# A kernel whose gate tiles get their Silu from the hyperbolic tangent, and whose Fourier row buffers share three rooms

## The chip, the cores and the metric

The kernel runs on one core of a Trainium2 chip. A core has a matrix engine (TensorE, PE in the profile, with its weight loads shown apart as PEld), a vector engine (VectorE, DVE), an engine for functions of single elements (ScalarE, ACT), a general one (GpSimd, POOL) and one that mostly issues transfers (SyncE, SP). Each runs its own instructions in order; semaphores join them. On-chip memory has 128 partitions (SBUF), and products are summed in PSUM banks. The metric is device time in microseconds of one execution; lower is better.

## The reference

Two sequences (prompt and sample) of 1024 rows and 1024 columns, fp32, go through one encoder layer. What matters here, for each sequence:

```python
xn = rmsnorm(x, g_pre)
p = xn @ w_in
fv, fg, hv, hg, mg = jnp.split(p, ...)
fz = jnp.fft.fftn(fz, axes=(1, 3), norm="ortho").real   # fz: fv in 4 groups of 256
y_f = (fz * jax.nn.silu(fg)) @ w_fourier_out
...                                                     # z: two gated long convolutions of hv
y_h = (z.astype(dt) * jax.nn.silu(hg)) @ w_hyena_out
g_f, g_h = jnp.split(jax.nn.sigmoid(mg + b_merge), 2, axis=-1)
out = (g_f * y_f + g_h * y_h) @ w_out
return x + rmsnorm(out, g_post)
```

`silu(x)` is x / (1 + exp(-x)), which is also x * (tanh(x/2) + 1) / 2. The long convolutions use filters of two orders that a small network makes: a product with sines, times an exponential decay, normed by the sum of absolute values, then taken to the frequency domain.

## The kernel before

Every fp32 matrix product is made of pairs: a number is split into a high part `h` and a rest `l`, both in the type float32r, and three products (h by h, l by h, h by l) are summed in PSUM (`mm3`; all products show up as L194). Weights that are split on the fly come in halves of 128 x 512: `wr` is read, ACT writes `h` (L761) and minus `h` (L762), and a transfer that adds, issued on POOL's queue, brings the weight again to make `l` (L763). `rooms` (L724) gives the halves of four tiles in turn a place: two pairs of rooms `wh`/`wl`, the room `draw`, and the room `draw2` of the pool `stage2`; in the last two a half is called `whl`.

The program has four stages. In the **Fourier stage** (0 to about 270 us) the sequences are normed, projected and transformed, one after the other. For each sequence four times a pair of row buffers, A and B (L458 and L459), is filled by DVE in four pieces each (L480 to L485) from the PSUM tile pQ and from Ps and Pm, copies of pP that ACT makes (L475, L476). POOL's queue then writes A and B to memory as `d_fz` (L486, L487). A and B have one buffer each, so the next pair waits for this transfer to end. In the first sequence the same places hold the first two input rows (L317). Ps, Pm and another small tile, `sev`, lie last in this stage's pool `ff`.

In the **filter stage** (about 225 to 720 us, begun while the Fourier stage ends) the filters' taps are made (L619 on: pft and the norm pn on PE, `ex` with Exp and Abs on ACT, T on DVE) and taken to the frequency domain (pXf). In between, `spill_gate` (L792) projects the gates: pairs of PSUM tiles pin0 and pin1 of 48 products of 512 columns in all. Section 0, the Fourier gate, is multiplied at once by `fz`, read back from `d_fz`; other sections are copied. The result goes to memory (`d_g`).

In the **convolution stage** (to about 1740 us) each channel block is projected, transformed, multiplied and transformed back; for some blocks the second gate is read back from `d_g` into `sg` and put through Silu (L1008). The table `cinv` of the inverse transform is read (L940) on POOL's queue when the Fourier stage's rooms are free. In the **block stage** (to the end) the output projections are made; its order is written by hand.

The order in the other stages is set by the program's scheduler: it simulates all instructions with a table of costs and puts each where the simulated engines are free. So an edit in one place can move work far away. The rooms of a pool follow one another in memory, and a pool that is closed gives its memory to the next ones, which wait for its last use.

Of the kernel before, what the change touches and what calls it, by code (L numbers as in the profile page):

```python
# [9 lines left out]
F32 = mybir.dt.float32  # L10
F32R = mybir.dt.float32r
I32 = mybir.dt.int32
AF = mybir.ActivationFunctionType
# [3 lines left out]
P = 128  # L17
D = 1024
# [143 lines left out]
class K:  # L162
# [143 lines left out]
    def norm(self, b, px, pf):  # L306

        nc, a = self.nc, self.a  # L310
        ss = px.tile([P, 8], F32, tag="ss", name=f"ss{b}")
        self.rs = rs = px.tile([P, 8], F32, tag="rs", name=f"rs{b}")
        self.diag = dg = px.tile([P, 8, P], F32, tag="dg", name=f"dg{b}", bufs=1)
        self.xs = []
        for m in range(8):
            if b == 0 and m < 6:
                x = pf.tile([P, D], F32, tag=("fA", "fB", "ee0", "ee1", "oo0", "oo1")[m], name=f"x0_{m}", bufs=1)  # L317
            else:
                x = px.tile([P, D], F32, tag="x", name=f"x{b}_{m}", bufs=3)
            nc.sync.dma_start(x, a[f"x{b}"][m * P:(m + 1) * P, :])  # L320
            self.xs.append(x)
            sq = px.tile([P, D], F32, tag="xg", name="sq", bufs=2)
            self.squared = nc.scalar.activation(sq, x, AF.Square, accum_out=ss[:, m:m + 1])
            if m % 4 == 3:
                q = slice(m - 3, m + 1)
                self.rstd(px, rs[:, q], ss[:, q], 4)
                for j in range(m - 3, m + 1):
                    self.scaled = nc.vector.tensor_scalar(dg[:, j], self.ident, rs[:, j:j + 1], None, op0=MUL)
# [57 lines left out]
    def fourier_half(self, b, half, W, fo, px, pf, begun={}):  # L386

        nc = self.nc
        WE, WO = W

        def pair(shape, tag, bufs=1):
            return [pf.tile(shape, F32R, tag=f"{tag}{i}", name=f"{tag}{i}", bufs=bufs) for i in range(2)]
        EE, OO = pair([P, 4, 260], "ee"), pair([P, 4, 256], "oo")
        for e, (W_, n, X_) in enumerate(((WE, 260, EE), (WO, 256, OO))):
            for m in range(4):
                p = begun.get((e, m))
                if p is None:
                    p = self.psum("mm", 4, f"pfv{e}")
                    for k in range(8):
                        self.pfv(p, e, m, k, W, fo)  # L400
                self.split(X_[0][:, m], X_[1][:, m], p[:, :n], "dve", "act")
                if e == (b + half == 0):

                    if m == 0:
                        p5 = self.psum("X", 2, "pfx")[0:36, :260]
                    for k in (2 * m, 2 * m + 1):
                        for i in range(2):
                            self.mm(p5, fo["x5"][:, k], WE[i][:, k], k + i == 0, k + i == 8)

        X5, XX, PX = fo["x5t"], fo["xx"], fo["px"]  # L410
        nc.scalar.copy(X5[0:36], p5)
        self.sub("dve", X5[32:36], p5[32:36], X5[32:36])

        EX = fo["ex"]
        for i in range(2):
            for g in range(2):
                nc.vector.tensor_copy(EX[i][:, :, g:g + 33:32], EE[i][:, :, 130 * g + P:130 * g + P + 2])
        for g in range(2):
            nc.vector.tensor_copy(XX[0:36, g:g + 33:32], X5[0:36, 130 * g + P:130 * g + P + 2])
        seq = fo["seq"].rearrange("p h (e m c) -> p h e m c", e=2, m=4)  # L420
        al = fo["alt"][:, b * 86:b * 86 + 86].unsqueeze(1).to_broadcast([P, 3, 86])

        def stage(np_, data, e, edge, out, tag):

            pe = self.psum(tag, 2, "pse")[0:np_, :258]
            po = self.psum(tag, 2, "pso")[0:np_, :258]
            for m in range(4):
                last = (edge is None and m == 1) or m == 3
                self.mm3(pe if m < 2 else po, data(m), (seq[:, 0, e, m], seq[:, 1, e, m]), m % 2 == 0, last)
                if m == 1 and edge is not None:  # L430
                    self.mm(pe.rearrange("p (a b) -> p a b", a=3), edge, al, False, True)
            ev = pf.tile([P, 258], F32, tag="sev", name="sev", bufs=1)[0:np_]
            st = pf.tile([P, 514], F32, tag="sst", name="sst", bufs=1)[0:np_]
            nc.scalar.copy(ev, pe)
            self.add("dve", st[:, 0:258], ev, po)
            if e == 0:
                self.sub("dve", st[:, 512:257:-1], ev[:, 0:255], po[:, 0:255])
            else:
                self.stt("dve", st[:, 512:257:-1], ev[:, 0:255], -1.0, po[:, 0:255])
            nc.vector.tensor_copy(st[:, 513:514], st[:, 0:1])  # L440
            if len(out) == 2:
                self.split(out[0], out[1], st, "dve", "act")
            else:
                nc.scalar.copy(out[0][0:34], st)
                self.sub("dve", out[0][32:34], st[32:34], out[0][32:34])
        ch, cx = fo["chan"], fo["chx"]
        vec = self.vec
        PP = []
        for g in range(2):
            cs = slice(130 * g, 130 * g + P)  # L450
            PP.append(pair([P, 514], "pp", 2))
            stage(P, lambda m: (EE[0][:, m, cs], EE[1][:, m, cs]), 0, X5[:, cs], PP[g], "TX"[g])
        stage(34, lambda m: (EX[0][:, m], EX[1][:, m]), 0, XX, [PX], "T")
        for g in range(2):
            Pp, Qp = PP[g], pair([P, 514], "qp")
            co = slice(P * g, P * g + P)
            stage(P, lambda m: (OO[0][:, m, co], OO[1][:, m, co]), 1, None, Qp, "XT"[g])
            A = pf.tile([P, 1026], F32, tag="fA", name="fA", bufs=1)  # L458
            B = pf.tile([P, 1026], F32, tag="fB", name="fB", bufs=1)  # L459
            gg = 2 * half + g  # L460
            for n in range(2):
                w = (258, 256)[n]
                ns = slice(258 * n, 258 * n + w)
                pr, qr = (Pp[0][:, ns], Pp[1][:, ns]), (Qp[0][:, ns], Qp[1][:, ns])
                pP = self.psum("X", 2, "pP")[:, :w]
                self.mm3(pP, (ch[:, 0, 0:P], ch[:, 1, 0:P]), pr, True, False)
                self.mm(pP, cx[:, 0, g, :], PX[:, ns], False, True)
                pQ = self.psum("X", 2, "pQ")[:, :w]
                self.mm3(pQ, (ch[:, 0, P:2 * P], ch[:, 1, P:2 * P]), qr, True, False)
                self.mm(pQ, ch[:, 0, 2 * P:3 * P], pr[0], False, False)  # L470
                self.mm(pQ, ch[:, 0, 2 * P:3 * P], pr[1], False, False)
                self.mm(pQ, cx[:, 1, g, :], PX[:, ns], False, True)
                Ps = pf.tile([P, 258], F32, tag="fPs", name="fPs", bufs=2)
                Pm = pf.tile([P, 258], F32, tag="fPm", name="fPm", bufs=1)
                nc.scalar.copy(Ps[:, :w], pP)  # L475
                nc.scalar.activation(Pm[:, :w], pP, AF.Copy, scale=vec[:, 11:12])  # L476
                t0 = 258 * n
                w = (258, 255)[n]
                r = slice(0, w)
                self.stt("dve", A[:, t0:t0 + w], pQ[:, r], vec[:, 10:11], Ps[:, r])  # L480
                self.add("dve", B[:, t0:t0 + w], pQ[:, r], Pm[:, r])
                w = (258, 254)[n]
                r = slice(0, w)
                self.stt("dve", A[:, 1024 - t0:1024 - t0 - w:-1], pQ[:, r], vec[:, 11:12], Ps[:, r])
                self.stt("dve", B[:, 1024 - t0:1024 - t0 - w:-1], pQ[:, r], vec[:, 12:13], Pm[:, r])  # L485
            nc.gpsimd.dma_start(self.d_fz[b][2 * gg], A[:, 0:1024])  # L486
            nc.gpsimd.dma_start(self.d_fz[b][2 * gg + 1], B[:, 0:1024])  # L487

# [303 lines left out]
    def spill_gate(self, b, sec, ct, ws):  # L792
# [4 lines left out]
        for n in range(2):  # L797
            s = slice(512 * n, 512 * n + 512)
            t = self.wp.tile([P, 512], F32, tag="gt", name="gt", bufs=3)
            if sec:  # L800
                nc.scalar.copy(t, ps[n])
            else:
                f = self.wp.tile([P, 512], F32, tag="gt", name="fz", bufs=3)
                nc.sync.dma_start(f, self.d_fz[b][ct][:, s])
                nc.scalar.activation(t, ps[n], AF.Silu)
                self.mul("dve", t, t, f)
            nc.sync.dma_start(self.d_g[b][sec][ct][:, s], t)


# [707 lines left out]
```

## Time and profile before

| | us |
|---|---|
| three executions | 2432.15, 2436.44 (median), 2437.8 |
| the profiled execution | 2433.46 |
| its span in the trace | 2431.7 |
| busy: PE | 2365.3 (97%) |
| busy: DVE | 1984.6 (82%) |
| busy: ACT | 1182.4 (49%) |
| busy: POOL | 452.5 (19%) |

The spans and windows below are in microseconds from the span's start. A row of the timeline gives the start, the duration, the engine, the line, the operation with output and inputs, and in brackets how long the engine was idle before it and what ended that. "Granted clock" is the share of TensorE's full clock that the chip allowed in a window. A busy PE is not always a PE at its peak, so the distance from one product to the next is looked at as well.

### The profile page before, as it was taken

What the parts mean: (1) busy time and instruction counts of PE and PEld (TensorE: products, weight loads), DVE (VectorE), ACT (ScalarE), POOL (GpSimd) and SP (SyncE); (2) the same over time, 40 slices, a digit from 0 to 9 for tenths busy, and PEclk for the clock granted to TensorE, in tenths of its full rate; (3) what the DMA queues carried; (4) which work ended last, traced back from release to release, by engine and by line L of the source; (5) the groups of instructions that cost most, each with busy time, mean ns of one, the idle gap of its engine ahead of it and who ended that gap; (6) DMA issues with size and microseconds to landing.
All of it is one profiled execution on the core that took longest, in us unless ns stands there. A gap on an engine that the chain in (4) does not pass through costs nothing. (4 is left out here: it accounts for less than half of the span.)

```text
span 2431.7 us, 37263 instructions
## 1 busy us (share of the span) xinstructions
PE 2365.3 (97%) x13006; PEld 2052.9 (84%) x13006; DVE 1984.6 (82%) x3840; ACT 1182.4 (49%) x2224; POOL 452.5 (19%) x568
## 2 busy tenths in 40 slices
PE   5998999999989999999999999999999999999998
PEld 5988888888878888888888888888878888888786
DVE  7687577777768999999899999997666687777777
ACT  5545677766765444434232332333344475656543
POOL 1331111111122222221025544410000000101000
PEclk9999999999989999999999999999999999999999
DMA  8546877777768667766455666554546687888744
GB/s 320 166 165 209 244 199 207 200 201 196 217 186 239 194 199 202 205 177 186 146 181 193 211 218 215 192 170 135 207 150 228 211 301 253 268 269 231 219 156 156
DMA packets 262981, 499.65 MB, mean 205 GB/s; under 512 B 26551, under 2 KB 90264, under 8 KB 262409
## 3 DMA queue, kind: packets, MB, share of 16 engines
q1 hardware_dynamic: 220076, 380.53, 47.6%
q0 software_dynamic: 42528, 116.72, 18.6%
q8 instruction: 102, 1.67, 0.3%
q14 instruction: 87, 0.70, 0.1%
q10 hardware_dynamic: 188, 0.02, 0.0%
HBM read 333.59 MB, written 167.77 MB: 206 GB/s over the span
## 5 line engine op out<-in xcount | busy, mean ns | idle before, releaser
L194 PE MATMUL pin<-xh,wh 128*128 128x512 f32 x1024 | 402.6, 394 | 1.7 <-DVE v L177 1.1
L194 PE MATMUL pin<-xl,wh 128*128 128x512 f32 x1024 | 402.5, 393 | 0.0
L194 PE MATMUL pin<-xh,wl 128*128 128x512 f32 x1024 | 401.8, 394 | 0.0
L194 PE MATMUL pin<-xh,whl 128*128 128x512 f32 x896 | 289.8, 393 | 0.0
L194 PEld LDWEIGHTS pin<-xh,wh 128*128 128x128 f32 x1024 | 193.7, 189 | 37.6 <-DVE v L177 1.4
L194 PEld LDWEIGHTS pin<-xh,wl 128*128 128x128 f32 x1024 | 193.6, 189 | 35.5
L194 PEld LDWEIGHTS pin<-xl,wh 128*128 128x128 f32 x1024 | 193.8, 189 | 34.9
L194 PE MATMUL pT<-cinv,yh 128*128 128x256 f32 x1024 | 192.6, 282 | 1.9 <-ACT xt L821 1.9
L194 PEld LDWEIGHTS pin<-xh,whl 128*128 128x128 f32 x896 | 166.5, 188 | 32.8
L194 PE MATMUL pin<-xl,whl 128*128 128x512 f32 x448 | 176.4, 394 | 0.0
L194 PEld LDWEIGHTS pT<-cinv,yh 128*128 128x128 f32 x1024 | 163.9, 190 | 11.0 <-ACT xt L821 2.3
L194 PE MATMUL pX<-bh,cfwd 128*128 128x256 f32 x768 | 160.5, 286 | 1.1 <-DVE t L181 1.0
L181 DVE TENSOR_TENSOR t<-pX,k 128x1024 f32<-128x1024 f32 x128 | 155.9, 1218 | 5.1 <-PE pX L194 2.6
L171 ACT CAST yh<-y 128x512 fp32r<-128x512 f32 x128 | 79.4, 620 | 149.5 <-DVE y L181 132.0
L194 PE MATMUL pT<-cinv,yl 128*128 128x256 f32 x512 | 145.2, 284 | 0.2 <-DVE yl L181 0.2
L171 ACT CAST bh<-b 128x512 fp32r<-128x512 f32 x144 | 88.8, 618 | 106.8 <-DVE b L181 76.6
L181 POOL TENSOR_TENSOR draw<-draw 128x256 f32<-128x256 f32 x96 | 112.1, 1168 | 108.9 <-DMA draw<-d_sh 38.3
L194 PEld LDWEIGHTS pX<-bh,cfwd 128*128 128x128 f32 x768 | 125.9, 190 | 4.7 <-DVE t L181 1.2
L181 DVE TENSOR_TENSOR bl<-b,bh 128x512 fp32r<-128x512 f32 x144 | 101.6, 707 | 22.3 <-ACT bh L171 22.1
L194 PE MATMUL pX<-bl,cfwd 128*128 128x256 f32 x384 | 109.7, 286 | 0.0
L177 DVE SCALAR_TENSOR_TENSOR x<-pin,wsh,x 128x512 f32<-128x512 f32 (+1 forms) x128 | 90.6, 743 | 11.4 <-ACT x L783 11.2
L194 PEld LDWEIGHTS pT<-cinv,yl 128*128 128x128 f32 x512 | 97.6, 191 | 2.5 <-DVE yl L181 0.4
(367 smaller groups left out, 6070.3 us busy)
## 6 DMA issues: line engine op xcount, KB each, us to landing
k<-d_k SPq DMA_DIRECT2D x128, 512.0 KB, 4.5
wr<-in_w_in SPq DMA_DIRECT2D x136, 256.0 KB, 3.6
d_g<-gt SPq DMA_DIRECT2D x92, 256.0 KB, 3.7
d_k<-kt SPq DMA_DIRECT2D x128, 128.0 KB, 3.0
d_k<-kt SPq DMA_DIRECT2D x64, 256.0 KB, 3.1
fz<-d_g SPq DMA_DIRECT2D x64, 256.0 KB, 5.4
wl<-in_w_in POOLq DMA_DIRECT2D x56, 256.0 KB, 5.3
whl<-in_w_in POOLq DMA_DIRECT2D x56, 256.0 KB, 5.1
```

Source lines behind the costliest of these rows:

```text
L171: self.rounded = nc.scalar.copy(h, src)
L177: self.nc.vector.scalar_tensor_tensor(out, a, s, b, op0=op0, op1=op1)
L181: return e.tensor_tensor(out, a, b, op=op)
L194: return self.nc.tensor.matmul(out, lhsT, rhs, start=start, stop=stop, skip_group_check=shared)
```

## The change

```diff
--- before.py
+++ after.py
@@ -314,7 +314,7 @@
         self.xs = []
         for m in range(8):
             if b == 0 and m < 6:
-                x = pf.tile([P, D], F32, tag=("fA", "fB", "ee0", "ee1", "oo0", "oo1")[m], name=f"x0_{m}", bufs=1)
+                x = pf.tile([P, D], F32, tag=("fAB", "fAB", "ee0", "ee1", "oo0", "oo1")[m], name=f"x0_{m}", bufs=3 if m < 2 else 1)
             else:
                 x = px.tile([P, D], F32, tag="x", name=f"x{b}_{m}", bufs=3)
             nc.sync.dma_start(x, a[f"x{b}"][m * P:(m + 1) * P, :])
@@ -455,8 +455,8 @@
             Pp, Qp = PP[g], pair([P, 514], "qp")
             co = slice(P * g, P * g + P)
             stage(P, lambda m: (OO[0][:, m, co], OO[1][:, m, co]), 1, None, Qp, "XT"[g])
-            A = pf.tile([P, 1026], F32, tag="fA", name="fA", bufs=1)
-            B = pf.tile([P, 1026], F32, tag="fB", name="fB", bufs=1)
+            A = pf.tile([P, 1026], F32, tag="fAB", name="fA", bufs=3)
+            B = pf.tile([P, 1026], F32, tag="fAB", name="fB", bufs=3)
             gg = 2 * half + g
             for n in range(2):
                 w = (258, 256)[n]
@@ -802,8 +802,9 @@
             else:
                 f = self.wp.tile([P, 512], F32, tag="gt", name="fz", bufs=3)
                 nc.sync.dma_start(f, self.d_fz[b][ct][:, s])
-                nc.scalar.activation(t, ps[n], AF.Silu)
-                self.mul("dve", t, t, f)
+                nc.scalar.activation(t, ps[n], AF.Tanh, scale=0.5)
+                self.stt("dve", t, t, 1.0, ps[n], ADD, MUL)
+                self.stt("dve", t, t, 0.5, f, MUL, MUL)
             nc.sync.dma_start(self.d_g[b][sec][ct][:, s], t)
```

The row buffers and the first two input rows have one tag, `fAB`, with three buffers instead of two tags with one each. The tiles of the pool behind them lie 4128 bytes per partition higher. In the gate tiles of section 0, ACT computes tanh(p/2) instead of silu(p); DVE then makes (t + 1) * p, with p from PSUM, and t * 0.5 * fz, where it made one product before. The Silu of the convolution stage stays.

The matrix products are the same in number and kind, and the program has 7 instructions ACT_TABLE_LOAD, where it had 25. The scheduler puts many instructions elsewhere. Three places follow.

POOL at the end of the Fourier stage, before, the numbers being those of the program's tiles (`whl_3612` is the second half of the second gate tile; `d_fz1` the rows of the second sequence):

```order
L763 DMA whl_3582<-in_w_in 128x512
L763 DMA whl_3612<-in_w_in 128x512
...
L486 DMA d_fz1_0_101<-fA_2827 128x1024
L487 DMA d_fz1_1_102<-fB_2828 128x1024
L763 DMA whl_3965<-in_w_in 128x512
L763 DMA wl_4004<-in_w_in 128x512
L486 DMA d_fz1_2_103<-fA_2895 128x1024
L487 DMA d_fz1_3_104<-fB_2896 128x1024
L763 DMA wl_4035<-in_w_in 128x512
L940 DMA cinv_4071<-in_c_inv 128x6144
L763 DMA whl_4284<-in_w_in 128x512
```

And in the changed program:

```order
L763 DMA whl_3582<-in_w_in 128x512
...
L763 DMA wl_3659<-in_w_in 128x512
L763 DMA wl_3690<-in_w_in 128x512
L763 DMA whl_3937<-in_w_in 128x512
L486 DMA d_fz1_0_101<-fA_2827 128x1024
L487 DMA d_fz1_1_102<-fB_2828 128x1024
L486 DMA d_fz1_2_103<-fA_2895 128x1024
L487 DMA d_fz1_3_104<-fB_2896 128x1024
L941 DMA cinv_4073<-in_c_inv 128x6144
L763 DMA whl_3612<-in_w_in 128x512
```

The transfer for `whl_3612` stood ahead of the second sequence's row buffers, and stands behind the last of them and behind `cinv`. The places of the tiles in memory show why: `sev`, Ps and Pm lay below the room `draw2`, and now overlap it.

PE behind the last pQ of the Fourier stage (`pQ_2922`), before: 40 projection products of other tiles stand between the first pft and pn (the first and the last two are shown):

```order
L194 MATMUL pQ_2922<-px_281,chx_287 128x256
L194 MATMUL pft_3040<-w3s_2993,hid_2985 128x256 x2
L194 MATMUL pin1_3655<-xh0_5_3069,wl_3688 128x512
L194 MATMUL pin1_3655<-xh0_6_3074,wh_3687 128x512
...
L194 MATMUL pin0_3933<-xl0_6_3075,whl_3965 128x512
L194 MATMUL pin0_3933<-xh0_6_3074,whl_3965 128x512
L652 MATMUL pn_3057<-acc_3001,ones_73 128x128
L653 MATMUL pn_3057<-ones_73,acc_3001 128x2
```

And in the changed program:

```order
L194 MATMUL pQ_2922<-px_281,chx_287 128x256
L194 MATMUL pft_3040<-w3s_2993,hid_2985 128x256 x2
L652 MATMUL pn_3057<-acc_3001,ones_73 128x128
L653 MATMUL pn_3057<-ones_73,acc_3001 128x2
L194 MATMUL pft_3104<-w3s_3095,hid_2985 128x256 x2
L194 MATMUL pft_3116<-w3s_3095,hid_2985 128x256 x2
L194 MATMUL pft_3104<-w3s_3095,hid_2985 128x256 x2
L194 MATMUL pft_3116<-w3s_3095,hid_2985 128x256 x2
L194 MATMUL pin0_3580<-xh0_4_3064,whl_3612 128x512
L194 MATMUL pin0_3580<-xl0_4_3065,whl_3612 128x512
L194 MATMUL pin1_3581<-xh0_4_3064,whl_3612 128x512
L194 MATMUL pin1_3581<-xl0_4_3065,whl_3612 128x512
```

Four products with the high part of `whl_3612` stand among the taps; behind them come four and one of pXf, the next filter's spectrum, and then the other twenty products with `whl_3612`, ten for each of pin0 and pin1, which need its low part too. Before, 90 projection products stood between `pQ_2922` and that spectrum.

ACT near the end of the filter stage, where the convolution stage's first gates come back from memory, before (`ex_7541` belongs to the last filter but one):

```order
L640 ACTIVATE ex_7541<-dec_7509,vec_68 128x256 x2
L1008 ACT_TABLE_LOAD
L1008 ACTIVATE sg_9154<-sg_9154 128x512
L171 CAST bh_7598<-b2_7589 128x512
L761 CAST wh_8677<-wr_8679 128x512
L171 CAST bh_7609<-b1_7590 128x512
L1008 ACTIVATE sg_9790<-sg_9790 128x512
```

And in the changed program (`ex_7908` and `ex_7921` belong to the last filter):

```order
L640 ACTIVATE ex_7908<-dec_7876,vec_68 128x256 x2
L801 COPY gt_8357<-pin0_8295 128x512
L171 CAST bh_7965<-b2_7956 128x512
L171 CAST bh_7976<-b1_7957 128x512
...
L1009 ACT_TABLE_LOAD
L1009 ACTIVATE sg_9166<-sg_9166 128x512
L640 ACT_TABLE_LOAD
L640 ACTIVATE ex_7921<-dec_7876,vec_68 128x256 x2
L1009 ACT_TABLE_LOAD
L1009 ACTIVATE sg_9170<-sg_9170 128x512
L695 ACTIVATE kt2_7999<-pXf_7988,th_69 128x128
```

The table loads and Silus of the first `sg` tiles stood ahead of the casts bh of the last filter but one; now they stand one filter later, behind two of the casts bh and between two Exp. On PE, between the pn that precedes the last filter's taps and its last pft, 49 projection products stood and 78 stand; the convolution stage starts its first product with 1632 of the projections' products done instead of 1702.

## The prediction

> **What bounds the kernel now.** I read the busy time by windows first, because the mean over the span mixes stages. Its columns are the stretch, then busy time (instructions) of PE, PEld, DVE, ACT and POOL, the granted clock, the DMA share and GB/s.
>
> ```profile
> 180.00:240.00 60.00, 52.28 (x381) 49.07 (x380) 43.86 (x94) 34.63 (x69) 13.14 (x18) 0.94 0.60 195
> 240.00:660.00 420.00, 420.00 (x2262) 362.47 (x2261) 308.62 (x789) 293.36 (x643) 55.03 (x66) 1.00 0.76 209
> 660.00:720.00 60.00, 51.55 (x242) 42.67 (x241) 45.07 (x113) 38.51 (x81) 12.66 (x19) 0.89 0.71 199
> 715.00:1740.00 1025.00, 1020.80 (x6034) 903.59 (x6033) 942.83 (x1698) 372.56 (x660) 281.22 (x332) 1.00 0.62 191
> 1380.00:1440.00 60.00, 60.00 (x364) 53.51 (x364) 59.67 (x108) 17.96 (x33) 33.61 (x37) 1.00 0.65 215
> ```
>
> The filter stage (240 to 660), where the gate tiles are made, is PE's: 420.00 of 420.00 us busy at full clock, with ACT at 293 and DVE at 309. Time is lost at its two ends: 7.7 us without PE work in 180 to 240 and 8.5 in 660 to 720, both with a clock below 1. The view of waits names what ended the idle time there (total, times, longest); first row from 200 to 240, the others from 672 to 722:
>
> ```profile
> PE pQ L194 <- DVE fB L177: 6.1, 1, 6.1
> PE pXf L194 <- ACT bh L171: 3.7, 1, 3.7
> PE pft L194 <- DVE T L181: 3.6, 3, 2.4
> PE pin L194 <- DVE v L177: 1.1, 1, 1.1
> ```
>
> So the change can move time only where PE idles now, or where it makes PE idle anew.
>
> **The gate's arithmetic: 0.** These are the groups by line:
>
> ```profile
> L640 ACT ACT_TABLE_LOAD x11 | 14.1, 1283 | 0.1
> L805 ACT ACT_TABLE_LOAD x8 | 10.3, 1283 | 0.1
> L805 ACT ACTIVATE gt<-pin 128x512 f32<-128x512 f32 x16 | 9.6, 597 | 0.1
> L177 DVE SCALAR_TENSOR_TENSOR x<-pin,wsh,x 128x512 f32<-128x512 f32 (+1 forms) x128 | 90.6, 743 | 11.4 <-ACT x L783 11.2
> L181 DVE TENSOR_TENSOR gt<-gt,fz 128x512 f32<-128x512 f32 x48 | 33.2, 692 | 17.8 <-ACT gt L805 13.1 <-DMA fz<-d_fz 3.5
> ```
>
> Now 25 loads of ACT's function table are made; the listing of the changed program has 7, since Tanh needs no load beside the filters' Exp. The 18 that go are 18 x 1283 ns = 23.1 us of ACT. DVE gets one scalar_tensor_tensor more for each of 16 halves; the nearest row with a PSUM operand of 128x512 is 743 ns, and the second one takes the place of the multiply of 692 ns: 16 x (743 + 743 - 692) = 12.7 us. Both lie below PE's 420 of 420: ACT's 293 falls, DVE's 309 grows to about 321. The PSUM bank is released by DVE instead of ACT, some 0.7 us later; four banks turn and half a tile of 24 products takes 5.5 us (0.23 us each, the pitch shown further down), so this hides as well. Without that cover the DVE work would cost 12.7 us. I take 0, between -2 and +3.
>
> [...]
>
> **The row buffers: -4.** The second pair of the second sequence, DVE and PE in order of time (start, duration, and in brackets the idle time before and its releaser), then two windows:
>
> ```profile
> 215.30 0.49 DVE L177 SCALAR_TENSOR_TENSOR fA<-pQ,vec,fPs 128x258 f32<-128x258 f32 x1 [4.23 <-DMA d_fz<-fA]
> 217.68 0.43 DVE L181 TENSOR_TENSOR fB<-pQ,fPm 128x258 f32<-128x258 f32 x1 [1.89 <-DMA d_fz<-fB]
> 218.96 1.01 PE L194 MATMUL pQ<-qp,chan 128*128 128x256 f32 x3 [6.09 <-DVE fB L177]
> 215.00:220.00 5.00, 1.04 (x5) 1.04 (x6) 1.70 (x4) 1.00 (x2) 0.00 (x0) 0.53 0.77 270
> 220.00:225.00 5.00, 4.17 (x26) 3.58 (x26) 3.88 (x9) 4.27 (x9) 1.05 (x2) 0.79 0.37 137
> ```
>
> PE waits 6.09 us for a PSUM bank that DVE cannot empty, because A and then B still wait for their old contents to be written out. With three rooms the second A has a free one. The second B takes the first A's room, so it still needs that transfer, which let A start at 215.30; B then starts behind it instead of at 217.68. That is 2.4 us for certain. If the room is free before PE gets there, all 6.09 goes, with the slow clock behind it (1.05 us by 5 x 0.21 in the second window): 7.1. Work queued on ACT behind the Pm copy (the hidden layer's and the taps' casts, then x5t) starts earlier too, but some of it waits for weights. I take -4 of (-2.4, -7.1).
>
> **The fourth weight room: +19.** The Fourier pool grows by 4128 bytes, and its last tiles (sev, Ps, Pm) now lie on the room `draw2`, which was free before. The second half of the second gate tile, whl_3612, cannot be filled until the stage's last read of Pm. In the changed order its accumulating transfer stands on POOL's queue behind the last two row buffers and behind `cinv`. That queue before, the last pQ on PE, and two answers on transfers from 270 to 300 and 240 to 330:
>
> ```profile
> 268.09 0.28 PE L194 MATMUL pQ<-px,chx 128*128 128x256 f32 x1
> 270.45 0.56 POOL L487 DMA_DIRECT2D d_fz<-fB  x1
> 277.45 0.55 POOL L940 DMA_DIRECT2D cinv<-in_c_inv  x1 [4.27 <-DMA d_fz<-fB]
> 277.99 0.92 POOL L763 DMA_DIRECT2D whl<-in_w_in  x1
> cinv<-in_c_inv POOLq DMA_DIRECT2D x1, 3072.0 KB, 12.9
> DMA to landing us min/median/max: 4.3/6.0/14.2
> ```
>
> Before, a weight half is issued at the same place, 277.99; nothing on PE needs it soon: 90 products of tiles whose weights are there stand between the last pQ and the next filter's spectrum. Now four stand there, and the twenty that follow need the late half's low part. From the end of the last pQ (268.4) to the issue is 9.6 us, and to its landing 23.8 us with the longest landing of 14.2 (the one behind cinv has that neighbour) or 15.6 with the median of 6.0. PE has in between, by the changed order, 18 products pft and two pn, four with the high half and five of pXf: about 4 us at 0.23 us for 512 columns and half of that for 256. Idle time is then 11.6 to 19.8 us. The restart is slow: thirteen products at 0.43 us instead of 0.23 (rows of the next part) add 2.6. Bounds +14 and +22; since the neighbour cinv is the same, I take +19. Whether DVE and ACT go on with the taps meanwhile does not pay PE back at once: it was already full from 240 to 660.
>
> [...]
>
> **The end of the filter stage: -12.** ACT and PE in order of time:
>
> ```profile
> 672.42 0.64 ACT L1008 ACTIVATE sg<-sg 128x512 f32<-128x512 f32 x1 [2.79 <-DMA sg<-d_g]
> 676.92 1.28 ACT L1008 ACT_TABLE_LOAD   x1 [1.05 <-DMA sg<-d_g]
> 678.75 0.60 ACT L171 CAST bh<-b 128x512 fp32r<-128x512 f32 x1
> 679.41 0.54 PE L194 MATMUL pXf<-bh,cfwd 128*128 128x256 f32 x1 [3.74 <-ACT bh L171]
> 681.03 0.63 PE L194 MATMUL pin<-xh,wl 128*128 128x512 f32 x1
> 681.45 0.63 PE L194 MATMUL pin<-xh,wh 128*128 128x512 f32 x1
> 706.09 0.51 PE L194 MATMUL pft<-w3s,hid 128*128 128x256 f32 x2 [2.42 <-DVE T L181]
> 711.37 0.80 PE L194 MATMUL pin<-xh,wh 128*128 128x512 f32 x1 [1.07 <-DVE v L177]
> 711.96 0.63 PE L194 MATMUL pin<-xl,wh 128*128 128x512 f32 x1
> 712.39 0.63 PE L194 MATMUL pin<-xh,wl 128*128 128x512 f32 x1
> 717.29 0.39 PE L194 MATMUL pin<-xh,wl 128*128 128x512 f32 x1
> 717.53 0.39 PE L194 MATMUL pin<-xh,wh 128*128 128x512 f32 x1
> ```
>
> Two losses. At 675.7 a table load and a Silu of the conv stage sit on ACT ahead of the cast bh, waiting for a reload from memory: 3.7 us of idle time, and eight products at 0.43 instead of 0.23 us (1.6). From 702 to 717 the last filter's taps leave PE without other work: 3.6 + 1.1 us idle, and thirteen slow products (2.6), with some 2 more for pft and pXf at half clock. Together 5.3 + 9.3 = 14.6 us. In the changed order the Silu comes one filter later and behind the casts bh, so the first 5.3 go; and between the pn ahead of the last filter and its last pft stand 78 products of projections where 49 stood: 29 x 0.23 = 6.7 us of cover. I take 5.3 + 6.7 = 12: -12, between -5 (only the first goes) and -15 (both go).
>
> **The conv stage: -4.** At its first product 1632 in-projection products are done, where 1702 were: 70 x 0.23 = 16 us of PE work move behind it. Most of this is paid there one for one, and the earlier start cancels it. Only what fills PE's idle time there is a gain: 4.2 us by the window 715 to 1740. In parts DVE sets the pace (59.67 of 60 us), which speaks for filling. The blocks after 1740 are ordered by hand and stay. I take -4, between 0 and -6.
>
> **Sum.** 0 - 4 + 19 - 12 - 4 = -1 us. The durations are of an execution of 2433.46 us (span 2431.7), which lies 3 us below the median 2436.44; the forecast is 2436.44 - 1 = 2435 us, its own range 2431 to 2441.
>
> **The rivals.**
>
> *Faster: the new stall is short.* The transfer lands by the median row, so the room costs +14; A and B give -7, the end -14, the conv stage -4: -11, 2425 us. For it: fewer other weight halves are in flight at that place. Against it: cinv's 3 MB, 12.9 us, go just ahead.
>
> *Slower: the late weight half costs all of it, and is not paid back.* One mechanism, at the last pQ: +22, while ACT still waits for the reloaded gate among the last taps, so that the end gives only -6 and the conv stage nothing; A and B -2: +14, 2450 us. It decides once the end of the filter stage gives back less than 10 us. For it: the changed order keeps table load and Silu, now ahead of the last Exp. Against it: 29 more products beside them.
>
> *ACT sets the pace of the filter stage after all.* Then the 23.1 us of table loads would come out, 2413 us. Against it are 420.00 of 420.00 us and a clock of 1.00. [...]
>
> *The rooms don't do what they say:* B still waits as long, so the first term is 0: 2439 us, within the forecast's own range.
>
> **How the numbers follow.** A measurement of this kernel tells 0.2%, 4.9 us, from no change. Chances: forecast (with the rooms that don't help) 0.36, short stall 0.31, late half 0.28, ACT 0.05. Faster 0.31 + 0.05 = 0.36, same 0.36, slower 0.28. The range takes in both neighbours' times nearly whole: 2422 to 2450.
>
> **What would show it.** Right: no wait of PE for fB over 4 us near 215; one wait of PE for the transfer whl of 11 to 20 us, 5 to 10 us after the last pQ, with a clock near 0.5 behind it; the window before the conv stage with under 4 us of idle time; 7 table loads; the filter stage full otherwise. Wrong: no wait for whl (then the time is under 2425), idle time on PE in 300 to 660 that DVE's gate operations end (the arithmetic is not hidden), or a last-taps stretch that still loses over 8 us.

## The result, and the profile after

The changed kernel takes 2428.82 us, median of 8 executions (2427.19 to 2429.65), beside 2436.76 us of the kernel before (2432.15 to 2440.32): a ratio of 0.9968, with an interval of 0.9959 to 0.9977. Run again later beside 25 executions of the kernel before, it was 2428.06 against 2436.64, 0.9966 (0.9956 to 0.9977). It is faster by 0.32%, more than the 0.2% by which the prediction tells a change from none. The range (2422 to 2450) holds the time; the likeliest case, no change at 2435 with its own range of 2431 to 2441, does not.

The windows of the profile after, with columns as in the prediction, and the row of 240 to 300 of the kernel before below it:

```profile
180.00:240.00 60.00, 55.17 (x382) 51.01 (x381) 42.87 (x93) 33.32 (x65) 10.23 (x15) 0.94 0.64 208
240.00:300.00 60.00, 48.65 (x240) 41.02 (x239) 41.84 (x101) 33.16 (x78) 8.18 (x12) 0.86 0.70 208
300.00:660.00 360.00, 360.00 (x1945) 310.91 (x1945) 283.90 (x729) 238.81 (x549) 42.88 (x49) 1.00 0.75 200
660.00:720.00 60.00, 59.01 (x317) 50.72 (x316) 45.57 (x108) 39.46 (x84) 12.92 (x19) 1.00 0.86 240
715.00:1740.00 1025.00, 1024.40 (x6042) 906.54 (x6041) 946.84 (x1682) 371.40 (x653) 292.35 (x339) 1.00 0.63 193
```

```profile
240.00:300.00 60.00, 60.00 (x308) 51.12 (x307) 33.63 (x83) 36.25 (x79) 10.75 (x14) 1.00 0.85 251
```

PE's idle time fell from 7.7 to 4.8 us in 180 to 240, rose from 0 to 11.4 in 240 to 300, fell from 8.5 to 1.0 in 660 to 720, and from 4.2 to 0.6 in the convolution stage.

At the row buffers, DVE and PE after. The second B now waits for the first A's transfer, as foreseen, and PE waits 2.24 us instead of 6.09:

```profile
211.43 0.43 DVE L181 TENSOR_TENSOR fB<-pQ,fPm 128x258 f32<-128x258 f32 x1 [3.88 <-DMA d_fz<-fA]
212.76 0.63 PE L194 MATMUL pQ<-qp,chan 128*128 128x256 f32 x3 [2.24 <-DVE fB L177]
```

Behind the last pQ, PE and POOL after, and the transfer's time to landing:

```profile
261.34 0.28 PE L194 MATMUL pQ<-px,chx 128*128 128x256 f32 x1
266.51 0.80 PE L652 MATMUL pn<-acc,ones 128*128 128x128 f32 x2 [4.65 <-DVE acc L181]
275.08 0.50 PE L194 MATMUL pft<-w3s,hid 128*128 128x256 f32 x2 [1.87 <-DVE T L181]
277.62 0.80 PE L194 MATMUL pft<-w3s,hid 128*128 128x256 f32 x2 [2.04 <-DVE T L181]
283.04 1.22 PE L194 MATMUL pin<-xh,whl 128*128 128x512 f32 x2 [2.70 <-DMA whl<-in_w_in]
```

```profile
269.47 0.53 POOL L941 DMA_DIRECT2D cinv<-in_c_inv  x1 [4.35 <-DMA d_fz<-fB]
270.73 0.90 POOL L763 DMA_DIRECT2D whl<-in_w_in  x1 [0.73 <-ACT whl L762]
DMA to landing us min/median/max: 12.3/12.3/12.3
```

The late half landed 21.4 us after the last pQ (261.6 to 283.0). But PE waited for it only at the end, 2.7 us. Of the 18.7 us before, 8.6 went in waits for the next filter's norm and taps, each ended by DVE (4.65, 1.87 and 2.04 us), because no gate products stood between; the rest was work, most of it at half clock (granted 0.51 from 266.2 to 273.1 and 0.50 from 276.5 to 286.7).

Where the kernel stands at the stages' borders is read from the group pX<-bh, whose products are the convolution stage's transforms. The row gives durations (smallest, median, largest), then the first and the last start. The first rows are two profiles of the kernel before, the second one taken in a run of its own; then two of the changed kernel.

```profile
L194 PE MATMUL pX<-bh,cfwd x768: 274/283/387, 765.8 to 1705.4; 128*128 128x256 f32 x192
```

```profile
L194 PE MATMUL pX<-bh,cfwd x768: 274/283/419, 768.4 to 1713.0; 128*128 128x256 f32 x192
```

```profile
L194 PE MATMUL pX<-bh,cfwd x768: 274/283/365, 750.5 to 1702.0; 128*128 128x256 f32 x192
```

```profile
L194 PE MATMUL pX<-bh,cfwd x768: 274/283/365, 748.5 to 1701.6; 128*128 128x256 f32 x192
```

From these, with the estimated 16 us of products that moved behind the border:

| | before (two profiles) | after (two profiles) | change of the means, moved work taken out |
|---|---|---|---|
| start to first pX | 765.8, 768.4 | 750.5, 748.5 | -17.6 + 16 = -1.6 |
| first to last pX | 939.6, 944.6 | 951.5, 953.1 | +10.2 - 16 = -5.8 |
| last pX to the end of the span | 726.3, 724.4 | 725.9, 725.1 | 0 |

By the first profiles alone the middle row is +11.9 - 16 = -4.1. PE's idle time in this stage points the same way without the estimate: 4.2 us before and 0.6 after in the first profiles (715 to 1740), and in the second ones 7.7 and 2.2:

```profile
720.00:1740.00 1020.00, 1012.33 (x5995) 896.93 (x5994) 940.72 (x1684) 367.24 (x651) 276.31 (x332) 1.00 0.62 190
```

```profile
720.00:1740.00 1020.00, 1017.84 (x6012) 900.89 (x6012) 939.34 (x1671) 367.39 (x650) 283.83 (x337) 1.00 0.62 192
```

So most of the gain is in the convolution stage, whose code the change does not touch. The block stage is the same.

### The profile page after: what moved, and what is told of

Its sections match the earlier page's. It is cut to its first block, busy times and chain, and to the rows that moved or that the text cites. A ratio compares the mean times of both kernels' runs of the same rounds, so it can differ in the third digit from the quotient of the medians.

```text
span 2427.9 us, 37224 instructions
## 1 busy us (share of the span) xinstructions
PE 2365.4 (97%) x13006; PEld 2054.0 (85%) x13006; DVE 1998.9 (82%) x3856; ACT 1161.1 (48%) x2206; POOL 457.5 (19%) x568
## 4 chain that ended last, share of the span: by engine, by line
PE 85%; DMA 7%; issue 3%; DVE 2%; ACT 2%; POOL 1%; SPq 0%; DVEq 0%; POOLq 0%; ACTq 0%
PE pin L194 38%; PE pg L194 25%; PE pT L194 7%; PE pX L194 6%; PE pXf L194 3%; PE pfv L194 2%; DMA whl<-in_w_in 2%; DMA wl<-in_w_in 1%; PE pft L194 1%; PE tph L821 1%; DMA x<-in_x 1%; PE tpx L194 1%; POOL d_w L736 0%; DMA wfv<-in_w_fv 0%; DMA bl<-d_t 0%
## 5 line engine op out<-in xcount | busy, mean ns | idle before, releaser
L181 POOL TENSOR_TENSOR draw<-draw 128x256 f32<-128x256 f32 x96 | 117.9, 1228 | 113.5 <-DMA draw<-d_sh 38.1
L181 DVE TENSOR_TENSOR yl<-y,yh 128x512 fp32r<-128x512 f32 x128 | 93.5, 731 | 16.3 <-ACT yh L171 16.2
```

Source lines behind the costliest of these rows:

```text
L181: return e.tensor_tensor(out, a, b, op=op)
```

## The experiments

**The second profile of the kernel before.** No edit.

> The kernel before once more, for a second profile. Its executions spread from 2431 to 2442 us, those of the changed kernel from 2427 to 2430. Theory (the spread is short waits of PE, on which the clock gate halves the clock or not): against the first profile, any difference lies in waits and half-clock stretches between 215 and 1740 us, and the block stage after 1740 agrees within 1 us. Rival (transfers are slower in some executions): the stages differ all alike, the block stage too.

It took 2439.2 us, with a span of 2437.4 instead of 2431.7. The block stage is 1.9 us shorter; 2.6 us are lost before the first pX and 5.0 in the convolution stage. There PE waits, and at one place its products then take 0.41 us where they took 0.28. ACT and PE of this profile at two places, and the wait of the first profile at the first of them:

```profile
896.04 0.63 ACT L1008 ACTIVATE sg<-sg 128x512 f32<-128x512 f32 x1 [7.60 <-DMA sg<-d_g]
897.09 0.58 ACT L821 COPY xt<-tph 128x512 f32<-128x512 f32 x1
897.72 0.51 PE L194 MATMUL pT<-cinv,yh 128*128 128x256 f32 x2 [2.23 <-ACT xt L821]
898.06 0.28 PE L194 MATMUL pT<-cinv,yl 128*128 128x256 f32 x1
...
1537.98 1.27 ACT L783 ACTIVATE x<-pin,wsh 128x512 f32<-128x512 f32 x2 [2.72 <-DMA d_sh<-x]
1539.13 0.59 ACT L871 COPY T1s<-pT 128x512 f32<-128x512 f32 x1
1539.77 0.66 PE L820 MATMUL tph<-ident,eo 128*128 128x128 f32 x4 [2.05 <-ACT T1s L871]
1542.20 0.63 PE L194 MATMUL pT<-cinv,yh 128*128 128x256 f32 x2
1542.63 0.41 PE L194 MATMUL pT<-cinv,yl 128*128 128x256 f32 x1
```

```profile
PE pT L194 <- ACT xt L821: 1.9, 1, 1.9
```

Each time ACT's first instruction in order waits for a transfer: the reload of a gate, or the write-out of x, whose room it needs. The copy that PE wants stands behind it, though its own input is there. After 2.05 us of idle time a product of 256 columns then takes 0.41 us instead of 0.28. In the first profile the wait at the second place was 0.4 us, and no half clock followed; the wait at the first place was nearly as long as here, so it is no part of the difference. PE's order is the same in both profiles, so the starts of the same products can be compared. The second profile is 0.9 us behind at the first product pfv<-we,eh (33.7 beside 32.8), 2.6 us at the last one (197.3 beside 194.7), and still 2.6 us at the first pX; it is 5.0 us behind at 1499.8, after a wait of 1.1 us for T1s, and 7.6 us behind the second place above. So the theory held for the convolution stage. It failed in two smaller points: the first 2.6 us are lost ahead of 215 us, and the block stage differs by 1.9 us where 1 was expected. The spread of the kernel before (2431 to 2442 us in 28 executions) has places such as these; two profiles can't show that there are no others.

**Each half of the change alone.** First the rooms (the diff's first two pieces, without the third):

> The three shared rooms for A and B, with Silu and one multiply in the gate tiles as before (25 table loads). Theory (the rooms move the work, the gate's arithmetic is hidden below PE): within 3 us of the changed kernel, about 2429, with the same idle time of PE from 240 to 300 (about 11 us) and no wait of 6 us for fB. Rival (the table loads that went are the gain): no gain here, 2436 or, with the late weight half, up to 2445.

Then the tanh (the third piece alone):

> Tanh and two DVE operations in the gate tiles, with A and B in one room each as before (9 table loads). Theory: the time of the kernel before, 2436 within 3 us, with PE's wait of about 6 us for fB and about 8 us of idle time from 660 to 720. Rival (the arithmetic is the gain): 2429, and the idle time from 660 to 720 gone.

The rooms alone: 2435.69 us, ratio 0.9997 (0.9988 to 1.0005). The tanh alone: 2438.64, 1.0002 (0.9991 to 1.0013). Neither half is faster. For the tanh the theory held: PE waits 6.5 us for fB and idles 10.0 us from 660 to 720. For the rooms it fell: their window 240 to 300 has 48.41 us of PE work, as foreseen, and 660 to 720 has 60.00, but the time is that of the kernel before. Is it then the table loads? The next two say no.

**The function alone, in two fixed orders.** In the changed kernel and in the kernel with the rooms alone:

```diff
-                nc.scalar.activation(t, ps[n], AF.Tanh, scale=0.5)
+                nc.scalar.activation(t, ps[n], AF.Silu, scale=0.5)
```

> The changed kernel with the function Silu written for Tanh and nothing else, so the gate tiles hold other numbers; the order on PE, DVE, POOL and SP is that of the changed kernel, instruction by instruction, and ACT gets 27 table loads instead of 7, 20 x 1.283 = 25.7 us more of ACT. Theory (hidden below PE): within 2 us of the changed kernel, 2429. Rival (ACT's time counts): 5 us slower or more, up to 2454 if nothing is hidden.

```diff
-                nc.scalar.activation(t, ps[n], AF.Silu)
+                nc.scalar.activation(t, ps[n], AF.Tanh)
```

> The kernel with the rooms alone, with the function Tanh written for Silu and nothing else, so the gate tiles hold other numbers; the order on all engines is that of the kernel with the rooms alone, and ACT has 5 table loads instead of 25, 25.7 us less. Theory (only the order matters, the loads are hidden): 2435.7 within 2 us. Rival (the loads cost about 7 us in this order): 2429.

The changed order with 20 table loads more: 2430.63 us, 0.9975 (0.9966 to 0.9984). The rooms' order with 20 fewer: 2433.46, 0.9995 (0.9985 to 1.0004). The loads, by line, in the changed order with Silu:

```profile
L640 ACT ACT_TABLE_LOAD x12 | 15.4, 1283 | 0.2
L805 ACT ACT_TABLE_LOAD x10 | 12.8, 1283 | 0.2
L1009 ACT ACT_TABLE_LOAD x2 | 2.6, 1283 | 0.0
```

25.7 us of ACT are worth 0.07% in the changed order and 0.02% in the other by these ratios (1.7 and 0.5 us), less than the intervals can tell from nothing. The second median is 2.2 us below that of the rooms alone, but the executions of the kernel before that ran beside it were lower by as much (2435.5 instead of 2437.56). Both kernels stay with their order. What separates 2429 from 2436 is the order of the instructions, not what the gate tile computes. PE's order is the same with either function, so the tanh helps only in that its second DVE operation makes the scheduler choose another order.

In the rooms' order (profile of the kernel with Tanh in it), ACT and PE:

```profile
1001.51 0.63 ACT L1008 ACTIVATE sg<-sg 128x512 f32<-128x512 f32 x1 [10.21 <-DMA sg<-d_g]
1003.03 0.62 ACT L171 CAST yh<-y 128x512 fp32r<-128x512 f32 x1
1003.70 0.50 PE L194 MATMUL pT<-cinv,yh 128*128 128x256 f32 x2 [2.55 <-ACT yh L171]
1531.54 0.77 PE L820 MATMUL tph<-ident,eo 128*128 128x128 f32 x4 [2.21 <-ACT T1s L871]
```

The same kind of wait stands there, at 1004 and 1532 us. They too come and go: the profile of the rooms alone, in the same order, has no wait for yh, and none over 0.8 us for T1s. The first profile of the changed kernel has no wait of PE over 0.4 us in this stage:

```profile
PE tph L821 <- ACT xt L822: 0.4, 1, 0.4
PE pT L194 <- ACT xt L822: 0.2, 1, 0.2
```

**The late fourth room.** First alone, in the kernel before, by an unused tile:

```diff
+            if b == 0 and m == 2:
+                pf.tile([P, 1026], F32, tag="spare", name="spare", bufs=1)
```

> The kernel before with an unused tile of 4104 bytes in the Fourier stage's pool: A and B keep one room each, Silu stays, but sev, Ps and Pm lie on the room draw2 as in the changed kernel. Theory (the overlap alone moves the gate tiles' order): the stall behind the last pQ (about 11 us of idle time from 240 to 300) and no more than 2 us of idle time from 660 to 720, with PE's wait of about 6 us for fB near 215 kept: 3 to 5 us above the kernel with the rooms alone, about 2440. Rival (the third room moves the order): the time and windows of the kernel before, 2437.

2436.51 us, 0.9998 (0.9987 to 1.0009). PE has 48.74 us of work in 240 to 300 and 60.00 in 660 to 720: the overlap alone, with no third room, makes the stall and takes the loss at the filter stage's end away, and in the time the two cancel.

```profile
240.00:300.00 60.00, 48.74 (x230) 40.61 (x229) 39.06 (x96) 34.18 (x77) 8.90 (x12) 0.80 0.69 207
660.00:720.00 60.00, 60.00 (x313) 51.32 (x313) 45.17 (x111) 39.18 (x81) 13.24 (x19) 1.00 0.84 239
```

The third room is seen beside it; the last pQ here, and in the kernel with the rooms:

```profile
263.16 0.28 PE L194 MATMUL pQ<-px,chx 128*128 128x256 f32 x1
```

```profile
260.20 0.28 PE L194 MATMUL pQ<-px,chx 128*128 128x256 f32 x1
```

It is worth 3 us there. PE's wait for fB near 215 is 3.8 us here, where about 6 was expected, and 0.9 with the rooms. The whole came out nearer to the kernel with the rooms than the 3 to 5 us expected (the interval reaches 0.11%, 2.7 us, to each side).

Then the rooms and the tanh without an early use of draw2, in two ways:

```diff
-        n = self.turn = (self.turn + 1) % 4
+        self.turn += 1
+        n = (0, 1, 2, 0)[self.turn - 4] if self.turn < 8 else (self.turn + 1) % 4
```

> The changed kernel, with the late room draw2 left out of the first round of weight rooms: the second half of the second gate tile takes a wh/wl room, and the turn goes on from there. Theory (the late fourth room takes PE's cover away behind the last pQ): idle time of PE from 240 to 300 falls from 11.4 us to under 5, and the time falls by 5 to 10 us, to about 2421. Rival (the cover is only moved: gate products used here are missing among the last filters' taps): the window 660 to 720 loses again what is gained, 2427 to 2431.

```diff
-        n = self.turn = (self.turn + 1) % 4
+        self.turn += 1
+        n = 0 if self.turn == 7 else self.turn % 4
```

> The changed kernel with draw2 left out of the first round, by taking wh/wl once more in its place, and the round after that starting as it would have: no late half is used early. The order behind the last pQ is that of the kernel before, with 1702 projection products ahead of the convolution stage. Theory (cover used here is missing later): no idle time from 240 to 300, about 8 us again from 660 to 720, 2431 to 2436. Rival (the late room is a net loss): about 2421.

The first: 2426.66 us, 0.9963 (0.9949 to 0.9977). The second: 2432.76, 0.9994 (0.9984 to 1.0003). Their windows 240 to 300 and 660 to 720, of the first and of the second:

```profile
240.00:300.00 60.00, 54.84 (x263) 45.80 (x262) 36.79 (x91) 33.25 (x76) 9.84 (x13) 0.91 0.71 213
660.00:720.00 60.00, 57.08 (x297) 48.82 (x296) 43.82 (x112) 38.15 (x82) 14.18 (x21) 0.94 0.79 229
```

```profile
240.00:300.00 60.00, 58.58 (x306) 49.91 (x305) 33.40 (x83) 32.72 (x75) 11.64 (x15) 1.00 0.78 224
660.00:720.00 60.00, 52.11 (x242) 43.18 (x241) 45.03 (x113) 38.43 (x80) 12.62 (x19) 0.89 0.70 198
```

With the stall gone, the loss at the filter stage's end comes back (7.9 us of idle time in the second kernel); with half of each, the first lies level with the changed kernel. So the first kernel's rival and the second one's theory held, which say the same: the cover is only moved. The late room is no net loss here, since its products stand among the last taps.

**The gate's reload taken off ACT.** If ACT, held by the reload of sg, is what PE waits for, then making that Silu when the gate is spilled should bring the gain without rooms and tanh. POOL then multiplies by what is reloaded, as before:

```diff
-            if sec:
+            if sec == 4 and b == 0:
+                nc.scalar.activation(t, ps[n], AF.Silu)
+            elif sec:
                 nc.scalar.copy(t, ps[n])
...
-                    nc.scalar.activation(sg, sg if early else ps[q], AF.Silu)
+                    if not early:
+                        nc.scalar.activation(sg, ps[q], AF.Silu)
```

In the kernel before:

> The kernel before with the same single edit: Silu of the second gate at the spill. A and B keep a room each and the Fourier gate its Silu; the order on PE is that of the kernel before but for some 20 rows. Theory (ACT held by the reload of sg makes PE wait for xt near 895 us, 1.9 to 3.5 us, and brings the half clock in some executions; another such wait at the last filters' taps, 3.7 us near 679, is the same reload): both waits go, 4 to 8 us faster, 2428 to 2433. Rival (ACT's waits are harmless): 2436 as before.

2427.69 us, 0.9965 (0.9953 to 0.9978): as fast as the changed kernel, with Silu, with A and B in one room each, with 37 table loads, and with nearly the order of before on PE. Its window 660 to 720, PE's waits there, its pX group, and its longest wait of PE in the convolution stage:

```profile
660.00:720.00 60.00, 55.24 (x284) 46.72 (x283) 48.82 (x124) 38.73 (x83) 14.13 (x21) 0.94 0.74 217
```

```profile
699.15 0.50 PE L194 MATMUL pft<-w3s,hid 128*128 128x256 f32 x2 [2.42 <-DVE T L181]
704.42 0.79 PE L194 MATMUL pin<-xh,wh 128*128 128x512 f32 x1 [1.07 <-DVE v L177]
```

```profile
L194 PE MATMUL pX<-bh,cfwd x768: 274/283/388, 757.9 to 1700.3; 128*128 128x256 f32 x192
```

```profile
PE tph L822 <- ACT T1s L873: 3.8, 2, 3.3
```

The wait of 3.7 us near 679 is gone, with the half clock behind it (0.51 granted from 679.4 to 682.7 before, products of 512 columns 0.43 us apart; from 678.8 to 680.7 here they start 0.23 us apart), and the first pX comes 7.9 and 10.5 us sooner than in the two profiles of before. The wait for xt near 895 is gone too, but another, of 3.3 us for T1s, has grown, and the convolution stage takes 942.4 us, no less than before. So the gain of this kernel is at the filter stage's end, and only the first of the two waits is shown to be worth its price.

In the changed kernel, and in the one with the fourth room later:

> The changed kernel, with the Silu of the second gate (section 4, first sequence) made when the projection is spilled, in place of the copy, so that ACT no longer stands behind the reload of sg in the convolution stage; POOL multiplies by the reloaded gate as before. 19 table loads. The order on PE is the changed kernel's but for some 80 rows. Theory (what the changed kernel gains in the convolution stage is that PE no longer waits behind an ACT held by transfers): little is left to gain here, 2426 to 2429. Rival (the order of the changed kernel is slow for another reason, sg counts): 2423 or less.

> The kernel with the fourth room left out of the first round, with Silu of the second gate at the spill as well. Theory: the short stall behind the last pQ (5 us of idle time) and no ACT held by sg: 2422 to 2426, below the changed kernel. Rival (the gains do not add up, since the order in the convolution stage is another than the changed kernel's): 2427 to 2430.

2429.11 us, 0.9972 (0.9963 to 0.9981), and 2427.91, 0.9967 (0.9951 to 0.9983). Neither is told apart from the changed kernel. For the first that was the theory: PE is busy all of 720 to 1740 us there, and had idled only 0.6 us of it before this edit. The second should have gained and did not, as its rival said. Nothing that ran is shown to beat the changed kernel; the kernel before with the gate at the spill equals it with one edit.

**The change once more.**

> The changed kernel once more, beside the three others and the same executions of the kernel before. Theory: 2427 to 2430, with a convolution stage (first to last pX) within 1 us of the first profile's 952.3 us, since its waits there are short. Rival (the first executions were lucky): a spread of 8 us or more and a median above 2431.

2428.06 us, 0.9966 (0.9956 to 0.9977), 2426.06 to 2432.7: the theory held for the time. Its pX row stands in the section on the result: 953.1 us beside 951.5, 1.6 us more where 1 was expected. This order isn't free of such waits either: the profile, of an execution of 2428.43 us, has one of 1.6 us for xt near 958. One execution of 11 was at 2432.7; no profile shows why.

## Why the prediction was right and where it was wrong

**What bounds the kernel.** Right: PE from 300 to 660 is full in both profiles, and time moved only where PE idled or came to idle.

**The gate's arithmetic, 0.** Right, and shown: 25.7 us of table loads put into the changed order, or taken out of the other, moved the time by 0.07% and 0.02%, less than the intervals can tell from nothing; the DVE operations left no wait of PE in the full windows. What the prediction didn't price is that the extra DVE operation changes the scheduler's order far away.

**The row buffers, -4.** Right in mechanism: the second B waits for the first A. The wait for fB falls by 3.9 us, the idle time of the whole window 180 to 240 by 2.9, and the third room is worth 3 us by the last pQ with and without it.

**The fourth weight room, +19.** Its place and its sign were right, and its price about 17.8: 11.4 us of idle time, and work at half clock. The clock granted after is 0.51 from 266.2 to 273.1 and 0.50 from 276.5 to 286.7, with 6.5 and 6.4 us of PE work in these stretches; half of that, 6.4, would not be needed at full clock. The prediction had 2.6 for this and 16.4 for the idle time. The landing ends the stretch, as foreseen, 21.4 us after the last pQ where 15.6 to 23.8 were reckoned. But PE's wait for it is only the last 2.7 us; before it, PE waits for taps that nothing covers, and works at half clock. The stated mark, a wait of PE for whl of 11 to 20 us, was wrong. That cover is the point is shown by its return: with it, the idle time is 1.4 us.

**The end of the filter stage, -12.** Right: idle time fell by 7.5 us, and the granted clock rose from 0.89 to 1.00. Of the 13 us at half clock that are gone (before, 0.51 is granted from 679.4 to 682.7 and 0.50 from 708 to 717), some 12 were work (eight and thirteen slow products, and the pft and pXf among them), worth about 6. Together that is -13.4. ACT's part is shown by the edit on the reload alone.

**The conv stage, -4.** Right by the profile that it was read from: -4.1 by the first profiles. By the means of two it is -5.8: the old order's waits behind an ACT that is held by transfers differ from execution to execution (0.4 or 2.05 us at one place), and behind the one of 2.05 us products took 0.41 instead of 0.28 us. One execution's idle time was not the whole price. Nor is it mere filling of PE's idle time, as I called it: the kernel with the rooms alone has the same 16 us of moved work and is no faster, so the order decides.

**The sum.** No single term failed by much. The first four terms made +3; the profiles show +0.7 by the first pair and -1.6 by the means of two. The step that failed is the one from profile to median: I added 3 us to both kernels alike, as if the spread stayed. The first profiled execution of before lies 3 us below its median, that of the changed kernel 0.8 above. Of the 7.9 us between the medians the first two profiles show 3.8, the means of two 7.2. That the other 4.1 us are waits of the old order which went is what the second profiles speak for; it is not shown for the executions without a profile.

**The range.** It held because it was drawn to take in both neighbours' times, 28 us wide, and not because the sum was good. The likeliest case, no change with a chance of 0.36, did not come; "faster", with 0.36, did.

**The rivals.** "Faster" by a short stall had the right side for a wrong reason: the stall was not short. "Slower" failed since the filter stage's end gave back more than 12 us. ACT as the limit and rooms that do nothing are excluded by the runs above.

What stays open: why the scheduler's order with both halves lets ACT's held instructions stand where PE isn't waiting, and with one half not. The rows show that it does; no run shows the rule. Nor is the whole distance to the rooms alone seen: that kernel's profile is of its fastest execution (2431.53 us), only 1.9 us above the changed kernel's, and the 4 us more of its median stand in no profile.

## What to carry to other kernels

Where a scheduler sets the order, price an edit by the order that it produces, and test the order apart from the arithmetic: the same order with the other function, and the other order with the same function, took two runs and settled what two half-changes alone left unclear. Here ACT waited 7.60 us for the reload of a gate, and the copy behind that Silu, for which PE idled 2.23 us, waited with it; move such an instruction to where its data already lie, as here the gate's function to the spill. And take two profiles of a kernel whose executions spread before a term is priced by the waits of one.

## What was not expected of the hardware

A wait of PE of 2.05 us was followed by products at nearly half the pace at one place (0.21 us apart instead of 0.12), and one of 2.23 us at another place was not: after 2.05 us of idle time at 1540 us products took 0.41 instead of 0.28 us in one profile of the kernel before, while after 2.23 us at 898 us, in the same profile, the next product of that size took 0.28 (rows in the first experiment). The slow products do not start right behind the wait: single products of 256 columns from 1540.2 to 1541.0 take 0.28 or 0.36 us, those from 1541.6 to 1544.1 take 0.41, and at 1545.2 one takes 0.28 again.

In the changed kernel the stretch at half clock near 266 us (0.51 granted from 266.2 to 273.1) follows 4.65 us of idle time.
